# Head of the first mixer: products of the first chunk from x not yet normalized, scaled when they are evicted; squares summed in pairs; the residual parts on VectorE alone

## The chip, the cores and the metric

The kernel runs on one core of a Trainium2 chip. A time is the device time of one execution in microseconds (us). One execution is also profiled, and the profile and trace that are read below come from it.

The core's engines work side by side, each through its own queue in order: PE (TensorE, matrix products, with PEld for its weight loads), DVE (VectorE), ACT (ScalarE), POOL (GpSimd) and SP, which here issues the DMA transfers. Matrix products are written to PSUM, of which there are eight banks.

## The reference

One inference step of a two-layer hybrid decoder: a Mamba-2 layer with an MLP, then a layer of sliding-window attention with an MLP. 1024 prompt tokens, 8x8 sample tokens and 16 meta tokens go through with shared weights. Only the start of the first layer matters here:

```python
def rmsnorm(x, w):
    xf = x.astype(jnp.float32)
    xf = xf * lax.rsqrt(jnp.mean(xf * xf, axis=-1, keepdims=True) + EPS)
    return (xf * w.astype(jnp.float32)).astype(x.dtype)

def mamba_mixer(h, conv_state, ssm_state, norm_w, w_in, conv_w, conv_b, dt_bias, ...):
    zxbcdt = rmsnorm(h, norm_w) @ w_in
    z = zxbcdt[..., :D_INNER]
    xbc = zxbcdt[..., D_INNER:D_INNER + CONV_DIM]
    dt_raw = zxbcdt[..., D_INNER + CONV_DIM:]
    ...
    for k in range(CONV_K):
        conv = conv + xpad[:, k:k + L] * conv_w[k]
    xbc = jax.nn.silu(conv)
    ...
```

The factor rsqrt(...) is one number per token. With features on the partitions and tokens on the columns, as the kernel has it, it is one number per column, the same for all features, and so it can be taken into x ahead of the product or into the product's columns afterwards.

## The kernel before

All 1104 tokens lie on the columns, in three chunks: `CH = [(0, 384), (384, 384), (768, 336)]`, chunk 2 being the last prompt tokens with the sample and meta tokens. Features lie on the 128 partitions in `KT = 8` tiles. Every product of fp32 matrices is made from three: each operand is split into a high part (cast to fp32r on ACT, `xh`, `wh`) and a low part (the rest, by a subtraction, `xl`, `wl`), and PE sums `wh xh + wh xl + wl xh` over k. So one unit of 128 output features takes 24 matmuls a chunk.

The mixer works group by group (8 groups). A group has four convolution units, B, C, x0 and x1. `conv_unit` loads a unit's weights into a `raw` buffer (two) and splits them into `w` buffers (six), and has an `xp` buffer (two) and an `fm` buffer (eight, which the pieces of x use too). `conv_mm` and `conv_mms` make the products in PSUM banks `g` (three), `conv_out` evicts them on ACT into `xp` and, scaled by the convolution's last weight, into `fm`. `conv_rest` does the rest of the convolution and its silu: small copies on POOL, three steps over the 80 tail columns and three over 1024 columns on DVE, Tanh on ACT. The dt product (`dt_product`) feeds `dt_path`, a chain on DVE and ACT whose results the scan (`ssd`) of every group needs.

The function `mixer` is the head that is changed. It loads chunk 2, the weights of B and C, chunk 0, chunk 1. For each chunk `sums_x` squares x on ACT and sums over the partitions with an f32 product against a matrix of 1/D on PE (chunk 2 adds the two squares of a pair on DVE first, chunks 0 and 1 give each square to PE); `rstd_x` makes exp(-0.5 ln(.)) on ACT; `norm_x` scales x in place on DVE (line 354), casts the high part on ACT (L355) and subtracts on DVE and POOL in turn (L357). `conv_mms` then makes B's and C's products of the chunk (L569 to L571), chunk 2 first. After the three chunks come the dt product (L436, L437), x0's products (L205 to L207, the helper `mm3`), `conv_rest` of B, C and x0, `dt_path` (its first transposes on PE at L466), x1, and the scan.

The order in every engine's queue is not written out: a planner orders the instructions by the program's order as priority and its own estimate of when each is ready. `issue_after(i)` adds an edge: what is traced in its block is queued behind instruction i on i's engine. Buffers of a pool go round: an instruction whose tile has no free buffer waits for the last reader of an older one. Besides `g`, PSUM holds one bank each of the tags `cb`, `st` and `tp` and two of `y`; the small SBUF pools are `n1` (five) and `n3` (two, where the rsqrt rows lie).

Of the kernel before, what the change touches and what calls it, by code (L numbers as in the profile page):

```python
# [3 lines left out]

# [5 lines left out]
F32 = mybir.dt.float32  # L10
F32R = mybir.dt.float32r
AF = mybir.ActivationFunctionType
ALU = mybir.AluOpType
# [4 lines left out]
P = 128  # L18
D = 1024
KT = D // P  # L20
# [8 lines left out]
CH = [(0, 384), (384, 384), (768, 336)]  # L29
CORD = [2, 0, 1]  # L30
# [112 lines left out]
class Kernel:  # L143
# [132 lines left out]
    def consts(self):  # L276
        nc, i = self.nc, self.i
        self.cp = cp = self.pool("const")
        self.ident = cp.tile([P, P], F32, name="ident")
        make_identity(nc, self.ident)  # L280

        ones = cp.tile([P, P], F32R, name="ones_r")
        nc.vector.memset(ones.bitcast(F32), 1.0 / D)
        self.ones_r, self.ones_d = ones, ones.bitcast(F32)
        eps = cp.tile([P, 3], F32, name="eps")
        self.eps1, self.eps4, warm = (eps[:, k:k + 1] for k in range(3))
        nc.vector.memset(self.eps1, EPS)

        nc.scalar.activation(out=warm, in_=self.eps1, func=AF.Ln)
        nc.vector.memset(self.eps4, 4.0 * EPS)  # L290
        self.nv = cp.tile([P, KT, 8], F32, name="nv")
        nc.sync.dma_start(out=self.nv, in_=i["nv"])

    def ncol(self, r):
        return self.nv[:, :, r]
# [26 lines left out]
    def sums_x(self, c, hp, tag, add=False):  # L322

        nc = self.nc
        n = CH[c][1]
        ms = self.psa.tile([P, 512], F32, tag=tag, bufs={"y": 2}.get(tag, 1), name="xms")
        for kp, h in enumerate(hp):
            sq = [self.n1("xsq")[:, :n] for _ in range(2)]
            for j in range(2):
                nc.scalar.activation(out=sq[j], in_=h[:, j], func=AF.Square)  # L330
            if add:
                nc.vector.tensor_tensor(out=sq[0], in0=sq[0], in1=sq[1], op=ALU.add)
            for j in range(1 if add else 2):
                nc.tensor.matmul(out=ms[:, :n], lhsT=self.ones_d, rhs=sq[j], start=(kp + j == 0),
                                 stop=(kp == 3 and (add or j == 1)))
        return ms[:, :n]

    def rstd_x(self, mss):
        rs = [self.n3()[:, 0, :ms.shape[1]] for ms in mss]
        for r, ms in zip(rs, mss):  # L340
            self.nc.scalar.activation(out=r, in_=ms, func=AF.Ln, bias=self.eps1)
        for r in rs:
            self.nc.scalar.activation(out=r, in_=r, func=AF.Exp, scale=-0.5)
        return rs

    def norm_x(self, c, hp, rs):

        nc = self.nc
        n = CH[c][1]
        w = self.ncol(5)  # L350
        xh, xl = self.xparts(c)
        for k in range(KT):
            h = hp[k // 2][:, k % 2]
            nc.vector.scalar_tensor_tensor(out=h, in0=h, scalar=w[:, k:k + 1], in1=rs, op0=ALU.mult, op1=ALU.mult)
            nc.scalar.copy(out=xh[:, k], in_=h)  # L355
            e = nc.gpsimd if k % 2 else nc.vector
            e.tensor_tensor(out=xl[:, k], in0=h, in1=xh[:, k].bitcast(F32), op=ALU.subtract)  # L357
        return xh, xl


# [197 lines left out]
                 [(xs[c][0][:, k, :n], xs[c][1][:, k, :n]) for k in range(KT)])  # L558
        self.conv_out(unit, c, pt)

    def conv_mms(self, units, c, xs):

        n = CH[c][1]
        pts = [self.gps() for _ in units]
        mm = partial(self.nc.tensor.matmul, skip_group_check=True)
        for k in range(KT):
            xh, xl = (x[:, k, :n] for x in xs[c])
            for (j, (wh, wl), *_), pt in zip(units, pts):
                mm(out=pt[:, :n], lhsT=wh[:, k], rhs=xh, start=(k == 0), stop=False)  # L569
                mm(out=pt[:, :n], lhsT=wh[:, k], rhs=xl, start=False, stop=False)  # L570
                mm(out=pt[:, :n], lhsT=wl[:, k], rhs=xh, start=False, stop=(k == KT - 1))  # L571
        for unit, pt in zip(units, pts):
            self.conv_out(unit, c, pt)

    def conv_out(self, unit, c, pt):
# [1376 lines left out]
    def mixer(self, c1):  # L1952

        nc = self.nc
        mp = self.pool("mixc", ctx=c1)
        self.sp = self.pool("sp", ctx=c1)
        self.psa = self.pool("psa", bufs=1, space=PSUM, ctx=c1)
        xs, fm = {}, {}
        hp = {2: self.load_h(2)}
        us = [self.conv_unit(0, nm) for nm in ("B", "C")]  # L1960
        hp[0] = self.load_h(0)
        hp[1] = self.load_h(1)
        self.mixer_consts(mp)
        ms2 = self.sums_x(2, hp[2], "cb", True)
        rs2 = self.rstd_x([ms2])[0]
        xs[2] = self.norm_x(2, hp[2], rs2)
        ms0 = self.sums_x(0, hp[0], "st")
        ms1 = self.sums_x(1, hp[1], "y")
        self.conv_mms(us, 2, xs)
        rs0, rs1 = self.rstd_x([ms0, ms1])  # L1970
        for c, rs in ((0, rs0), (1, rs1)):
            xs[c] = self.norm_x(c, hp[c], rs)
            self.conv_mms(us, c, xs)
        draw = self.dt_product(mp, xs)
        ux = self.conv_unit(0, "x0")
        fm["B"], fm["C"] = (self.conv_rest(u) for u in us)
        for c in CORD:
            self.conv_mm(ux, c, xs)
        fm["x0"] = self.conv_rest(ux)
        sums = self.dt_path(mp, draw)  # L1980
        next(sums)
        ux = self.conv_unit(0, "x1")
        for k, c in enumerate(CORD):
            if k == 1:
                next(sums, None)
            self.conv_mm(ux, c, xs)
        next(sums, None)
        fm["x1"] = self.conv_rest(ux)
        for g in range(G):
            gate = None  # L1990
            if g + 1 == G:
                y = [self.fm([P, T], "gy") for j in range(2)]
                space = lambda c: ((self.sp.tile([P, 1024], F32, tag="bm", bufs=1, name="gt") if c == 1 else
                                    self.cw.tile([P, T], F32, tag="th", bufs=1, name="gt"))[:, :768]
                                   .rearrange("p (j n) -> p j n", j=2))
                gate = self.gate_group(0, xs, y, space, lambda: self.fm([P, T], "gm"))
            for t in self.ssd(g, fm):
                for k in range({8: 2, 2: 1, 3: 1, 6: 1, 7: 1}.get(t, 0) if gate is not None else 0):
                    next(gate)
            if g + 1 < G:  # L2000
                fm = self.group_in(g + 1, xs)
        nc.sync.dma_start(out=self.o["conv"], in_=self.cvo)
        for _ in gate:
            pass
        return xs
# [68 lines left out]
```

## Time and profile before

| | |
|---|---|
| time, median of three executions | 2864.05 us (2859.41 to 2864.07) |
| profiled execution | 2867.18 us, of which its span (first to last instruction) is 2865.5 us |
| granted TensorE clock | 0.992 |
| PE busy | 2800.5 us (98%) |
| DVE busy | 2077.3 us (72%) |
| ACT busy | 1419.1 us (50%) |
| POOL busy | 472.0 us (16%) |
| DMA | 433.41 MB, 151 GB/s mean |

A row of a timeline gives start and length, engine, line of the kernel, operation, the tiles written and read with their shapes, how many instructions are merged, and in brackets the idle time of the engine before it and what released it. A row of a group gives busy time and the mean length in ns, then the idle time ahead of the group. Matmuls are pipelined, so the length of one contains latency; its price is the step from one start to the next. "L569" is line 569 of the kernel before.

### The profile page before, as it was taken

Reading aid. Unit: us, or ns where it says so; the run is one execution under the profiler, and the core shown is the slowest. Engines: PE = TensorE matmul, PEld = TensorE weight load, DVE = VectorE, ACT = ScalarE, POOL = GpSimd, SP = SyncE. Lnnn points to the kernel's source line nnn. Section 1 sums busy time; section 2 is a strip of 40 time slices with the busy share of each in tenths; the row PEclk is TensorE's granted clock in tenths of the full one; section 3 lists DMA queues with packets and bytes.
Section 4 is the critical chain, followed back from the end, with each engine's and each line's share of the span. In section 5 each row is a group of like instructions: output and inputs, shape, how many; then the busy total and the mean of one; then the engine's idle time right before and its main releaser. Section 6 shows DMA issues by size and latency. Waiting matters only on the chain.

```text
span 2865.5 us, 51402 instructions
## 1 busy us (share of the span) xinstructions
PE 2800.5 (98%) x19895; PEld 2697.7 (94%) x19895; DVE 2077.3 (72%) x3615; ACT 1419.1 (50%) x2742; POOL 472.0 (16%) x659
## 2 busy tenths in 40 slices
PE   8999999989999999999999999999999999999998
PEld 6999999979999999999999999988989999999997
DVE  6788888876778786666578875676687666567786
ACT  6555555554664265445344335555555455523333
POOL 3255555551000100000000022110110000000011
PEclk9999999999999999999999999999999999999998
DMA  4244444457655223533655523446553454533432
GB/s 139 77 133 124 122 124 124 125 142 249 244 204 184 88 94 130 178 132 131 248 192 181 187 94 92 165 170 245 175 194 105 143 174 152 219 115 127 143 114 70
DMA packets 219468, 433.41 MB, mean 151 GB/s; under 512 B 30729, under 2 KB 128393, under 8 KB 216649
## 3 DMA queue, kind: packets, MB, share of 16 engines
q1 hardware_dynamic: 219224, 430.14, 45.2%
q8 instruction: 156, 2.56, 0.4%
q14 instruction: 88, 0.71, 0.1%
HBM read 302.71 MB, written 128.32 MB: 150 GB/s over the span
## 4 chain that ended last, share of the span: by engine, by line
PE 84%; DVE 7%; DMA 5%; ACT 3%; issue 2%; POOL 0%; SPq 0%; DVEq 0%; ACTq 0%; POOLq 0%
PE g L205 11%; PE g L206 11%; PE g L207 11%; PE mc L205 4%; PE mc L207 4%; PE mc L206 4%; PE ma L205 4%; PE ma L207 4%; PE ma L206 4%; PE md L206 3%; PE md L207 3%; PE md L205 3%; PE mb L206 3%; PE mb L205 3%; PE mb L207 3%
## 5 line engine op out<-in xcount | busy, mean ns | idle before, releaser
L205 PE MATMUL g<-S,w 128*128 128x384 f32 (+2 forms) x1584 | 530.0, 335 | 3.7 <-DMA w<-ws_up 1.9
L206 PE MATMUL g<-S,w 128*128 128x384 f32 (+2 forms) x1584 | 531.3, 335 | 0.0
L207 PE MATMUL g<-S,w 128*128 128x384 f32 (+2 forms) x1584 | 527.2, 333 | 0.0
L1068 ACT CAST w<-s 128x384 fp32r<-128x384 f32 (+1 forms) x272 | 150.3, 557 | 318.0 <-PE mc L207 57.7
L205 PEld LDWEIGHTS g<-S,w 128*128 128x128 f32 x1584 | 298.4, 188 | 6.7 <-issue 3.4
L206 PEld LDWEIGHTS g<-S,w 128*128 128x128 f32 x1584 | 298.9, 189 | 3.0 <-issue 2.4
L207 PEld LDWEIGHTS g<-S,w 128*128 128x128 f32 x1584 | 299.4, 189 | 2.1 <-issue 1.7
L1319 POOL TENSOR_TENSOR hh<-hh,us 128x552 f32<-128x552 f32 (+1 forms) x24 | 42.4, 1788 | 1535.9 <-DVE us L1295 880.4
L205 PE MATMUL ma<-S,w 128*128 128x276 f32 (+1 forms) x808 | 234.3, 290 | 5.8 <-ACT A L1256 2.1
L206 PE MATMUL ma<-S,w 128*128 128x276 f32 (+1 forms) x808 | 234.0, 290 | 0.4 <-DVE S L1257 0.3
L207 PE MATMUL ma<-S,w 128*128 128x276 f32 (+1 forms) x808 | 234.1, 290 | 0.0
L1069 DVE TENSOR_TENSOR w<-s,w 128x384 fp32r<-128x384 f32 (+1 forms) x272 | 166.3, 615 | 77.8 <-ACT w L1068 77.8
L1068 ACT CAST w<-raw 128x384 fp32r<-128x384 f32 (+1 forms) x204 | 112.2, 556 | 177.0 <-PE mc L207 55.7
L171 ACT CAST w<-raw 128x1024 fp32r<-128x1024 f32 x96 | 100.7, 1049 | 136.0 <-PE g L206 47.4
L205 PEld LDWEIGHTS ma<-S,w 128*128 128x128 f32 x808 | 152.6, 189 | 6.7 <-ACT A L1256 2.2
L206 PE MATMUL g<-R,w 128*128 128x384 f32 (+2 forms) x480 | 158.3, 330 | 0.0
L205 PE MATMUL g<-R,w 128*128 128x384 f32 (+2 forms) x480 | 157.8, 329 | 0.0
L207 PE MATMUL g<-R,w 128*128 128x384 f32 (+2 forms) x480 | 157.7, 329 | 0.0
L172 DVE TENSOR_TENSOR w<-raw,w 128x1024 fp32r<-128x1024 f32 x96 | 121.5, 1266 | 45.2 <-ACT w L171 30.8
L206 PEld LDWEIGHTS ma<-S,w 128*128 128x128 f32 x808 | 152.9, 189 | 0.8 <-DVE S L1257 0.5
L207 PEld LDWEIGHTS ma<-S,w 128*128 128x128 f32 x808 | 152.8, 189 | 0.0
L205 PE MATMUL mc<-S,w 128*128 128x276 f32 (+1 forms) x512 | 148.1, 289 | 0.7 <-DVE rx L1098 0.7
(497 smaller groups left out, 8559.8 us busy)
## 6 DMA issues: line engine op xcount, KB each, us to landing
raw<-in_w_up_dram SPq DMA_DIRECT2D x64, 512.0 KB
raw<-in_w_in_dram SPq DMA_DIRECT2D x48, 512.0 KB
raw<-in_w_downs_dram SPq DMA_DIRECT2D x64, 384.0 KB
w<-ws_o SPq DMA_DIRECT2D x46, 512.0 KB
w<-ws_q SPq DMA_DIRECT2D x40, 512.0 KB
ab<-acs_d SPq DMA_DIRECT2D x64, 256.0 KB
S<-t_d SPq DMA_DIRECT2D x18, 828.0 KB
S<-t_e SPq DMA_DIRECT2D x18, 816.0 KB
```

Source lines behind the costliest of these rows:

```text
L171: nc.scalar.copy(out=wh, in_=raw)
L172: nc.vector.tensor_tensor(out=wl, in0=raw, in1=wh.bitcast(F32), op=ALU.subtract)
L205: mm(out=out, lhsT=wh, rhs=xh, start=(first and k == 0), stop=False)
L206: mm(out=out, lhsT=wh, rhs=xl, start=False, stop=False)
L207: mm(out=out, lhsT=wl, rhs=xh, start=False, stop=(k == n - 1))
L1068: self.last_hi = nc.scalar.copy(out=t[:, 0], in_=src).ins
L1069: self.last_lo = nc.vector.tensor_tensor(out=t[:, 1], in0=src, in1=t[:, 0].bitcast(F32), op=ALU.subtract).ins
L1319: e.tensor_tensor(out=to, in0=to, in1=uv, op=ALU.add)
```

## The change

- `ln_exp`, new, issues one load of the activation table that holds both Ln and Exp at the start of ACT's queue.
- `raw_x`, new, makes the high and low parts of chunk 2 from x times the norm's weight alone, without the rsqrt: Identity with a scale on ACT, one scalar_tensor_tensor on DVE, for each of the eight feature tiles.
- B's and C's products of chunk 2 are made from these parts in the two `y` banks (`held`) and are not evicted at once. When rs2 is there, DVE multiplies each by it into an `n1` tile, which `conv_out` reads in place of PSUM.
- All three chunks sum the pairs of squares on DVE before the f32 product. The sums lie in the banks `cb`, `st` and `tp`. Chunk 0 goes first; chunks 2 and 1 share one `rstd_x`.
- `norm_x` subtracts on DVE alone, and scaling k is queued behind subtraction k-2 on DVE.
- Chunk 2 is normalized after all for the later products, behind chunk 1's last subtraction on DVE.
- x0's products come before the dt product and in the order of chunks 0, 1, 2; `conv_rest` of B and C stands between them and the dt product.

```diff
@@ consts
+        self.ln_exp()
         nc.scalar.activation(out=warm, in_=self.eps1, func=AF.Ln)
@@
+    def ln_exp(self):
+        nc = self.nc
+        return nc.scalar.add_instruction(mybir.InstLoadActFuncSet(
+            name=nc.get_next_instruction_name(), engine=mybir.EngineType.Activation, act_func_set_id=6,
+            ins=[], outs=[])).ins
@@ sums_x
-        ms = self.psa.tile([P, 512], F32, tag=tag, bufs={"y": 2}.get(tag, 1), name="xms")
+        ms = self.psa.tile([P, 512], F32, tag=tag, name="xms")
@@
-    def norm_x(self, c, hp, rs):
-        nc = self.nc
-        n = CH[c][1]
+    def raw_x(self, c, hp):
+        nc = self.nc
         w = self.ncol(5)
         xh, xl = self.xparts(c)
         for k in range(KT):
             h = hp[k // 2][:, k % 2]
-            nc.vector.scalar_tensor_tensor(out=h, in0=h, scalar=w[:, k:k + 1], in1=rs, op0=ALU.mult, op1=ALU.mult)
-            nc.scalar.copy(out=xh[:, k], in_=h)
-            e = nc.gpsimd if k % 2 else nc.vector
-            e.tensor_tensor(out=xl[:, k], in0=h, in1=xh[:, k].bitcast(F32), op=ALU.subtract)
+            nc.scalar.activation(out=xh[:, k], in_=h, func=AF.Identity, scale=w[:, k:k + 1])
+            nc.vector.scalar_tensor_tensor(out=xl[:, k], in0=h, scalar=w[:, k:k + 1], in1=xh[:, k].bitcast(F32),
+                                           op0=ALU.mult, op1=ALU.subtract)
+        return xh, xl
+
+    def norm_x(self, c, hp, rs):
+        nc = self.nc
+        n = CH[c][1]
+        w = self.ncol(5)
+        xh, xl = self.xparts(c)
+        subs = []
+        for k in range(KT):
+            h = hp[k // 2][:, k % 2]
+            with self.tc.issue_after(subs[k - 2]) if k > 1 else nullcontext():
+                nc.vector.scalar_tensor_tensor(out=h, in0=h, scalar=w[:, k:k + 1], in1=rs, op0=ALU.mult, op1=ALU.mult)
+            self.last_cast = nc.scalar.copy(out=xh[:, k], in_=h).ins
+            subs.append(nc.vector.tensor_tensor(out=xl[:, k], in0=h, in1=xh[:, k].bitcast(F32), op=ALU.subtract).ins)
+        self.last_side = subs[-1]
         return xh, xl
@@
-    def conv_mms(self, units, c, xs):
+    def conv_mms(self, units, c, xs, pts=None):
         n = CH[c][1]
-        pts = [self.gps() for _ in units]
+        hold = pts is not None
+        pts = pts or [self.gps() for _ in units]
...
-        for unit, pt in zip(units, pts):
+        for unit, pt in zip(units, () if hold else pts):
             self.conv_out(unit, c, pt)
@@ mixer
-        ms2 = self.sums_x(2, hp[2], "cb", True)
-        rs2 = self.rstd_x([ms2])[0]
-        xs[2] = self.norm_x(2, hp[2], rs2)
-        ms0 = self.sums_x(0, hp[0], "st")
-        ms1 = self.sums_x(1, hp[1], "y")
-        self.conv_mms(us, 2, xs)
-        rs0, rs1 = self.rstd_x([ms0, ms1])
-        for c, rs in ((0, rs0), (1, rs1)):
-            xs[c] = self.norm_x(c, hp[c], rs)
-            self.conv_mms(us, c, xs)
+        xs[2] = self.raw_x(2, hp[2])
+        rs0 = self.rstd_x([self.sums_x(0, hp[0], "cb", True)])[0]
+        held = [self.psa.tile([P, 512], F32, tag="y", bufs=2, name="xy") for _ in us]
+        self.conv_mms(us, 2, xs, held)
+        ms2 = self.sums_x(2, hp[2], "st", True)
+        xs[0] = self.norm_x(0, hp[0], rs0)
+        self.conv_mms(us, 0, xs)
+        ms1 = self.sums_x(1, hp[1], "tp", True)
+        rs2, rs1 = self.rstd_x([ms2, ms1])
+        n = CH[2][1]
+        for unit, pt in zip(us, held):
+            t = self.n1("xy")[:, :n]
+            nc.vector.tensor_tensor(out=t, in0=pt[:, :n], in1=rs2, op=ALU.mult)
+            self.conv_out(unit, 2, t)
+        xs[1] = self.norm_x(1, hp[1], rs1)
+        self.conv_mms(us, 1, xs)
+        with self.tc.issue_after(self.last_side):
+            xs[2] = self.norm_x(2, hp[2], rs2)
+        ux = self.conv_unit(0, "x0")
+        for c in range(3):
+            self.conv_mm(ux, c, xs)
+        fm["B"], fm["C"] = (self.conv_rest(u) for u in us)
         draw = self.dt_product(mp, xs)
-        ux = self.conv_unit(0, "x0")
-        fm["B"], fm["C"] = (self.conv_rest(u) for u in us)
-        for c in CORD:
-            self.conv_mm(ux, c, xs)
         fm["x0"] = self.conv_rest(ux)
```

More of the change, by code (lines that the diff above doesn't have):

```diff
@@ L1 @@
-from contextlib import ExitStack, contextmanager
+from contextlib import nullcontext, ExitStack, contextmanager
 from functools import partial
@@ L342, in rstd_x @@
         for r in rs:
-            self.nc.scalar.activation(out=r, in_=r, func=AF.Exp, scale=-0.5)
+            self.last_exp = self.nc.scalar.activation(out=r, in_=r, func=AF.Exp, scale=-0.5).ins
         return rs
+    def raw_x(self, c, hp):
[8 more added lines that the diff above has]
+        return xh, xl
     def norm_x(self, c, hp, rs):
```

## The prediction

> **What bounds the kernel now.** I read the busy line of the page first, then the busy time by stage, then the order of time of the first 76 us, engine by engine. In the stage rows the columns are the length, then PE, PEld, DVE, ACT and POOL with instruction counts, the granted clock, the DMA share and GB/s.
>
> ```profile
> span 2865.5 us, 51402 instructions
> PE 2800.5 (98%) x19895; PEld 2697.7 (94%) x19895; DVE 2077.3 (72%) x3615; ACT 1419.1 (50%) x2742; POOL 472.0 (16%) x659
> 0.00:10.60 10.60, 4.33 (x7) 2.25 (x8) 2.49 (x8) 5.96 (x11) 4.35 (x27) 1.00 0.79 268
> 10.60:21.40 10.80, 6.18 (x19) 2.73 (x17) 9.12 (x13) 10.51 (x23) 3.91 (x4) 1.00 1.00 354
> 21.40:34.40 13.00, 13.00 (x64) 10.60 (x65) 7.83 (x13) 9.96 (x21) 5.27 (x7) 1.00 0.16 52
> 34.40:55.50 21.10, 18.11 (x98) 16.54 (x97) 14.91 (x26) 13.02 (x26) 11.07 (x16) 1.00 0.14 50
> 55.50:75.80 20.30, 20.30 (x123) 18.52 (x120) 13.96 (x14) 9.36 (x17) 3.52 (x8) 1.00 0.23 78
> 75.80:110.00 34.20, 34.20 (x217) 33.54 (x218) 26.98 (x44) 16.60 (x36) 4.84 (x12) 1.00 0.24 56
> 110.00:600.00 490.00, 489.94 (x3347) 449.92 (x3346) 402.58 (x693) 271.18 (x641) 261.19 (x371) 1.00 0.46 125
> 600.00:660.00 60.00, 52.31 (x356) 43.32 (x356) 43.45 (x99) 30.40 (x82) 30.33 (x37) 0.91 0.55 146
> ```
>
> PE is the bound, and from 55.5 to 600 us it never rests. So a microsecond by which PE's stream starts earlier in the head is a microsecond of the total, as long as what feeds PE afterwards keeps up. The head is what is left: up to 55.5 us PE is busy for 41.6 of 55.5 us, and part of that is slow or removable work. Its marks in order of time (start, length, engine and line, and in brackets the idle time before and its releaser):
>
> ```profile
> 4.56 1.78 ACT L330 ACTIVATE xsq<-xt 128x336 f32<-128x336 f32 x4 [2.26 <-DMA xt<-in_x_dram]
> 7.43 1.79 ACT L330 ACTIVATE xsq<-xt 128x336 f32<-128x336 f32 x4 [1.09 <-DMA xt<-in_x_dram]
> 9.55 1.04 ACT L171 CAST w<-raw 128x1024 fp32r<-128x1024 f32 x1 [0.33 <-DMA raw<-in_w_in_dram]
> 10.62 2.54 DVE L172 TENSOR_TENSOR w<-raw,w 128x1024 fp32r<-128x1024 f32 x2 [0.86 <-ACT w L171]
> 14.48 0.48 ACT L343 ACTIVATE n<-n 128x336 f32<-128x336 f32 x1
> 15.00 5.22 DVE L354 SCALAR_TENSOR_TENSOR xt<-xt,nv,n 128x336 f32<-128x336 f32 x8 [1.56 <-ACT n L343]
> 21.40 0.42 PE L570 MATMUL g<-S,w 128*128 128x336 f32 x1 [1.91 <-DVE S L357]
> 36.03 0.44 PE L570 MATMUL g<-S,w 128*128 128x384 f32 x1 [1.28 <-DVE dx L478]
> 40.76 0.44 PE L569 MATMUL g<-S,w 128*128 128x384 f32 x1 [0.60 <-ACT fm L584]
> 46.66 0.44 PE L570 MATMUL g<-S,w 128*128 128x384 f32 x1 [1.11 <-DVE S L357]
> 55.51 0.31 PE L436 MATMUL g<-S,w 128*64 128x336 f32 x1
> ```
>
> The first chunk (336 columns) has landed by 7.4 to 9 us, and B's weights are cast by 10.6. Yet its products run only from 21.4, because sum, Ln, Exp, scaling and split stand between. The products of the three chunks and the remaining sums then take until 55.5, where the dt product starts (L436).
>
> **The change part by part.** Prices of PE work first, from starts that follow each other:
>
> ```profile
> 21.66 0.32 PE L571 MATMUL g<-S,w 128*128 128x336 f32 x1
> 21.82 0.32 PE L570 MATMUL g<-S,w 128*128 128x336 f32 x1
> 25.57 0.81 PE L334 MATMUL xms<-xsq,ones_r 128*128 128x384 f32 x2
> 26.37 0.81 PE L334 MATMUL xms<-xsq,ones_r 128*128 128x384 f32 x2
> 55.16 0.34 PE L570 MATMUL g<-S,w 128*128 128x384 f32 x1
> L334 PE MATMUL xms<-xsq,ones_r 128*128 128x384 f32 x32 | 12.7, 495 | 2.7 <-ACT xsq L330 2.7
> L334 PE MATMUL xms<-xsq,ones_r 128*128 128x336 f32 x8 | 4.9, 760 | 6.3 <-DVE xsq L332 6.3
> ```
>
> A product of 336 columns steps by 0.155 us, one of 384 by 0.175 (two of them from 55.16 to the 55.51 above). A sum over squares is one f32 product, two records; from 25.57 to 26.37 there are one of these and one 336 product in 0.80, so it costs 0.645 (384), by columns 0.56 (336).
>
> *Raw products (raw_x, held).* For chunk 2, eight Identity activations take the place of the eight squares at 4.56 to 9.2, and eight DVE subtractions follow them; both are done by about 10. So PE starts at 9.55+1.04 = 10.6 with 48 products of 0.155, 7.4 us; C's cast and the second halves of both weights (13.2) come before PE needs them.
>
> *Sums paired.* Before, 20 f32 products: 4 for chunk 2, 8 each for the others. After, 12: 4x0.56+8x0.645 = 7.4 us of PE, of which none lies ahead of 10.6 any more. The eight extra additions go to DVE.
>
> *Chunks 0 and 1.* 96 products of 0.175 = 16.8 us, as before.
>
> *Cold start.* The first eight sum records, the narrower ones, average 760 ns, against 495x336/384 = 433 by columns of the later ones: 1.75 times slower, though the granted clock column says 1.00. They fill the 4.3 busy us ahead of 10.6, which were free. After the change the first PE work is on the path: 4.33x(1-1/1.75) = 1.9 us lost. Bounds: 0 if the slowness is only waiting between records, 4.3 if it lasts twice as long; I take 1.9, what the rows themselves give.
> The Trainium skill, "TensorE: Matmul & The Clock Gate" ("What's actually happening"), speaks against the change here: whatever is issued in roughly the first 3.4 us of matmul activity runs at half the clock. By it the loss is an estimated 1.7 us instead of 1.9; the rows agree in kind, the clock column does not show it.
>
> *The normalizing path.* Before, a chunk's parts alternate between DVE and POOL; after, all lie on DVE, 16 instructions a chunk in a fixed order.
>
> ```profile
> 28.91 6.60 DVE L354 SCALAR_TENSOR_TENSOR xt<-xt,nv,n 128x384 f32<-128x384 f32 x8 [5.17 <-ACT n L343]
> 39.81 4.32 DVE L354 SCALAR_TENSOR_TENSOR xt<-xt,nv,n 128x384 f32<-128x384 f32 x8 [1.47 <-ACT n L343]
> 44.16 4.62 POOL L357 TENSOR_TENSOR S<-xt,S 128x384 fp32r<-128x384 f32 x4
> 35.43 0.54 DVE L357 TENSOR_TENSOR S<-xt,S 128x384 fp32r<-128x384 f32 x1
> L357 DVE TENSOR_TENSOR S<-xt,S 128x384 fp32r<-128x384 f32 x8 | 7.3, 952 | 0.0
> ```
>
> The same eight scalings took 6.60 us with POOL's subtractions beside them and 4.32 before POOL's began at 44.16. So 0.54 each without POOL, and 0.54 for a subtraction: 1.08 per k, against six products of 0.175 = 1.05 on PE. Bounds 0.54 and 0.95 per instruction (DVE's mean beside POOL); I take 0.6, near the low end, since no such POOL work is left, plus a little for waiting on the cast.
> The Trainium skill, "SBUF — State Buffer" ("Who interferes with whom"), says that a DVE instruction with two SBUF inputs and a GpSimd one that reads SBUF exclude each other. By it the price is 0.54, and the two L354 rows agree; I keep 0.6.
>
> When does it start? Chunk 0 lands at about 14.0: ahead of its end 32+1344+1024+1536 KB (4.03 MB) are queued by their shapes, 2.84 MB have moved by 10.6 (268 GB/s), the rest at 354. Behind the last piece come its two squares (1.0) and what took chunk 2 from its last square (9.22) to its Exp's end (14.96), 5.7, less two weight casts (2.1) and the table load (1.3): 17.3, and 18 with PE's queue ahead of the last sum. DVE then has 32x0.6 = 19.2, four additions for chunk 1 (0.5 each), x0's weight subtraction (1.2), two scalings of the held products (1.0) and a pause of about 1 between the chunks (rs1 needs rs0's buffer, then Ln and Exp): 42.4.
>
> *Sum to the end of chunk 1.* PE: 10.6+1.9+7.4+7.4+16.8 = 44.1, with its own stalls on top: 0 (x0's first chunk fills them) to 6 (twice the 3.0 us of the rows at 36.03, 40.76 and 46.66). I take 2, as DVE ends at 42.4, just ahead. So 46.1 against 55.5: 9.4 us gained.
>
> *Table loads.* One load at the start takes the place of those between Ln and Exp:
>
> ```profile
> L343 ACT ACT_TABLE_LOAD x3 | 3.8, 1283 | 0.1
> L341 ACT ACT_TABLE_LOAD x2 | 2.6, 1283 | 0.0
> 62.50 1.13 ACT L606 ACTIVATE th<-fm 128x1104 f32<-128x1104 f32 x1 [1.10 <-DVE fm L603]
> ```
>
> Five of 1.28 us go; the first Tanh may need a new one. On rs0's chain two would have counted, but PE is busy with chunk 2 and sums until about 22 (10.6+1.9+7.4+2.6), so the gain is in the cover and counts as nothing; at the Tanh ACT idles 1.10.
>
> *x0 ahead of dt, normalizing chunk 2 late.* The dt product and x0 change places; same work. x0's load passes w_dt's on SP's queue: w_dt is needed 20 us later than x0, nothing lost. Chunk 2's true parts cost DVE 16x0.55 = 8.8, to 51; x0 reaches its third chunk at 46.1+8.4 = 54.5, so this is covered by 3 us. What is queued behind it on DVE is conv_rest of B (the first two rows are of the chain of waits: the dt product's last step and the transposes behind x0):
>
> ```profile
> 63.50 0.18 PE g L437
> 75.79 2.04 PE tp L466 x18
> 58.71 4.87 DVE L603 SCALAR_TENSOR_TENSOR fm<-xp,cv,fm 128x1024 f32<-128x1024 f32 x4
> 76.72 1.23 DVE L172 TENSOR_TENSOR w<-raw,w 128x1024 fp32r<-128x1024 f32 x1 [6.79 <-ACT w L171]
> ```
>
> Three tail steps (0.3 each) and three of 1.2: B's xp is free at 55.6, and only then can x0's evictions start (two xp buffers) and give back a PSUM bank. PE needs a bank again when x0's third chunk is through, at 54.5+3.7 = 58.2. Cover 2.6 us. DVE idled 6.8 us ahead of 76.72, so its backlog of some 7 us can be worked off. I put 0.4 for this passage, bounds 0 and 5.
>
> *Total.* 9.4-0.4 = 9.0. The profiled execution took 2867.2 us (span 2865.5), 3.1 above the median of 2864.05; so 2858 like it, 2855 as a median. With bounds: best 9.4+2+1.9 = 13.3 gained, worst 9.4-4-2.4-5 = -2.0.
>
> **The rivals.**
> *DVE becomes the bound.* If its instructions cost 0.82 (the contended L354 row), chunks 0 and 1 end at 18+26.2+5.2 = 49.4, chunk 2's parts at 61, B's conv_rest at 65.6, and the dt product, waiting for a bank, runs from 66.2 for its 8 us (55.5 to 63.7 before) to 74, where before both were through at 75.8: gain 2, time 2862. For it: DVE is at 72% over the run; against: the 4.32 row.
> *Later stages give it back.* Group 0's dt path and scan are chains through DVE, ACT and DRAM; with PE ahead, PE may wait where it did not. DVE is busy 26.98 of 34.2 us there. Then the gain shrinks to between 0 and 4: 2862. Against: PE waits nowhere from 55.5 to 600, and dt is also ready earlier. The stretch from 600 to 660 does have 7.7 us of idle PE, and the order of all queues is planned anew.
> *Slower: the bank ring locks.* x0 holds all three g banks until conv_rest of B, behind chunk 2's 16 instructions on DVE, lets go of xp; the dt product needs a bank. Past 58.2 us every microsecond of B's conv_rest is PE idle; it decides from 58.2+9.4 = 67.6, and to lose 0.2% it must end at 73.3. That takes 0.98 per DVE instruction over the 48 of three chunks (55.6+48x0.37), about the 952 mean beside POOL. With it 2871.
> *The table load does not take.* If Ln and Exp still load their tables, rs0 comes 2.6 us later, at 20.6, still ahead of 22, but DVE ends at 45 and 1 more us shows: 2856.
>
> **How the numbers follow.** Likeliest, 0.58: 2855, its own range 2851 to 2859. DVE-bound 0.14, given back 0.14, slower 0.09, table loads kept 0.05. About 0.2% (5.7 us) is what can be told from no change: faster means below 2858.3. Of the likeliest case nine tenths lie there, all of the kept loads, and little of the two 2862 cases: 0.52+0.05+0.03 = 0.60. Slower 0.09, the rest 0.31. The range 2849 to 2864 takes in the two middle rivals and leaves out the slow one and the best corner.
>
> **What would show it.** Right: L569 to L571 from about 10.6, the first of them slow; no L357 on POOL; 12 sums (24 records) at L334's successor; one table load ahead of the first Exp; the dt product behind x0, and the transposes after it (L466) at about 66 instead of 75.8. Wrong: PE idle between 22 and 58 above 6 us, DVE instructions in the norm above 0.7 us, or an idle PE waiting for ACT's eviction of x0 before the dt product; or the head ends 9 us earlier but the span does not.

## The result: 0.2% slower, and the profile after

| | changed kernel | before, beside it |
|---|---|---|
| time, median | 2868.09 us (2863.84 to 2873.16, 15 executions) | 2862.69 us (2855.85 to 2868.49, 15 executions) |
| ratio, 95% interval | 1.0022 [1.0014, 1.0029] | |
| profiled execution | 2865.91 us, span 2864.2, clock 0.992 | 2867.18 us, span 2865.5 |

The forecast was 2855, 9 us won; measured are some 4 to 6 us lost (a second series, below, gave 1.0013). The profiled execution of before happened to be one of its long ones, so the two spans say nothing; the medians and the place where time goes do. Lines of the changed kernel stand further down: L592 to L594 are L569 to L571 of before, L342 is L334, L376 to L378 are L354 to L357, L458 and L459 are L436 and L437, L603 to L607 are `conv_out`, L626 is L603, L1073 is L1050 and L1056 is L1033. In the experiments the lines stand up to five off these again (in e5 L348 and L350 are Ln and Exp, in e8 L1991 is the added products).

Two lines of the page of the changed kernel, and its busy time by stage, with the columns as in the prediction:

```profile
span 2864.2 us, 51383 instructions
PE 2791.4 (97%) x19879; PEld 2692.9 (94%) x19879; DVE 2083.2 (73%) x3645; ACT 1418.2 (50%) x2746; POOL 451.0 (16%) x647
```

```profile
10.60:21.40 10.80, 10.47 (x46) 8.98 (x47) 6.12 (x9) 7.89 (x17) 0.72 (x3) 1.00 0.98 351
21.40:34.40 13.00, 13.00 (x62) 10.31 (x62) 11.73 (x25) 11.12 (x26) 2.67 (x7) 1.00 0.15 52
34.40:55.50 21.10, 18.68 (x104) 17.59 (x103) 18.89 (x43) 14.91 (x33) 0.61 (x4) 1.00 0.16 52
55.50:75.80 20.30, 18.37 (x104) 15.87 (x103) 18.04 (x19) 11.19 (x18) 3.46 (x10) 0.92 0.23 76
2175.00:2200.00 25.00, 16.55 (x98) 16.25 (x97) 23.01 (x27) 14.21 (x20) 0.00 (x0) 0.80 0.27 88
```

PE is busy for 9.1 us less than before, and the head does start earlier: 10.47 of 10.8 us busy where it was 6.18. But from 55.5 to 75.8, where PE had never rested, it now lacks 1.9 us and its clock falls to 0.92. And at 2175 to 2200 us, in a stage that the change doesn't touch, PE stands for 8.45 of 25 us. The same stretch of before:

```profile
2175.00:2200.00 25.00, 24.94 (x168) 24.72 (x168) 25.00 (x28) 18.22 (x24) 0.00 (x0) 1.00 0.13 45
```

Counted at one mark after another, the lead over before is 2.9 us at the first scan (first row of L508 of before at 99.9 us, 97.1 after), 8.2 when the last `g` product before 2192 starts, and is gone when the first `ma` product follows (2191.5 before, 2192.0 after).

The head of the changed kernel in order of time, from its timelines:

```profile
10.59 0.65 PE L592 MATMUL xy<-S,w 128*128 128x336 f32 x1 [10.59 <-ACT w L171]
14.54 0.48 PE L594 MATMUL xy<-S,w 128*128 128x336 f32 x1
15.09 0.32 PE L593 MATMUL xy<-S,w 128*128 128x336 f32 x1
16.08 0.56 DVE L340 TENSOR_TENSOR xsq<-xsq 128x384 f32<-128x384 f32 x1 [0.59 <-ACT xsq L338]
20.43 0.81 PE L342 MATMUL xms<-xsq,ones_r 128*128 128x384 f32 x2
21.51 0.56 ACT L349 ACTIVATE n<-xms,eps 128x384 f32<-128x384 f32 x1
23.28 1.14 DVE L376 SCALAR_TENSOR_TENSOR xt<-xt,nv,n 128x384 f32<-128x384 f32 x2
39.45 0.61 PE L592 MATMUL g<-S,w 128*128 128x384 f32 x2 [2.21 <-ACT S L377]
46.52 0.56 DVE L378 TENSOR_TENSOR S<-xt,S 128x384 fp32r<-128x384 f32 x1
60.55 0.32 PE L207 MATMUL g<-S,w 128*128 128x336 f32 x1
60.75 1.04 ACT L171 CAST w<-raw 128x1024 fp32r<-128x1024 f32 x1 [4.80 <-PE g L206]
62.07 0.68 ACT L607 ACTIVATE fm<-g,cv 128x384 f32<-128x384 f32 x1
62.80 0.52 PE L458 MATMUL g<-S,w 128*64 128x336 f32 x1 [1.93 <-ACT fm L607]
66.19 0.36 PE L458 MATMUL g<-S,w 128*64 128x336 f32 x1
64.63 1.28 ACT L629 ACT_TABLE_LOAD   x1
```

PE starts at 10.59, and steps by 0.28 us until about 15. The last pair of chunk 0's squares is added by 16.64, but PE takes its four sums between the products of chunk 2, the last at 20.43, so the scaling starts at 23.28 instead of 18. At 60.7 x0 is through; then the dt product waits 1.93 us for a bank (2.1 from where its start was due), and its next 12 products step by 0.28 again instead of 0.155. Products at such a slow step are called cold below.

The place of the loss, first in the changed kernel, then in the one before (PE, then DVE; L1050 and L1073 evict a bank `g`):

```profile
2183.18 0.34 PE L207 MATMUL g<-S,w 128*128 128x384 f32 x1
2191.97 0.56 PE L205 MATMUL ma<-S,w 128*128 128x272 f32 x1 [8.45 <-DVE n L1073]
2196.18 0.30 PE L205 MATMUL ma<-S,w 128*128 128x272 f32 x1
2187.79 1.29 DVE L1056 TENSOR_TENSOR S<-X,S 128x1088 fp32r<-128x1088 f32 x1
2189.59 0.56 DVE L1073 SCALAR_TENSOR_TENSOR n<-g,acc 128x384 f32<-128x384 f32 x1
2191.26 0.56 DVE L1073 SCALAR_TENSOR_TENSOR n<-g,acc 128x384 f32<-128x384 f32 x1
```

```profile
2191.00 0.34 PE L205 MATMUL g<-S,w 128*128 128x384 f32 x1
2191.54 0.28 PE L205 MATMUL ma<-S,w 128*128 128x272 f32 x1
2198.07 0.55 DVE L1050 SCALAR_TENSOR_TENSOR n<-g,acc 128x384 f32<-128x384 f32 x1
```

Before, `ma` follows on the last `g` product at once; the last eviction at 2198 is of a bank that `ma` doesn't need. After, PE is through at 2183.4, but the two last evictions stand on DVE behind other work until 2191.8, and `ma` needs one of their banks. On top, the 18 products up to 2196.18 step by 0.23 instead of 0.125, 1.9 us more.

### The profile page after: what moved, and what is told of

The parts are those of the page before. It is cut to its first block, busy times and chain, and to the rows that moved or that the text cites. A ratio compares the mean times of both kernels' runs of the same rounds, so it can differ in the third digit from the quotient of the medians.

```text
span 2864.2 us, 51383 instructions
## 1 busy us (share of the span) xinstructions
PE 2791.4 (97%) x19879; PEld 2692.9 (94%) x19879; DVE 2083.2 (73%) x3645; ACT 1418.2 (50%) x2746; POOL 451.0 (16%) x647
## 4 chain that ended last, share of the span: by engine, by line
PE 85%; DVE 5%; DMA 4%; ACT 3%; issue 2%; SPq 0%; DVEq 0%; POOL 0%; ACTq 0%
PE g L205 11%; PE g L206 11%; PE g L207 11%; PE ma L205 4%; PE ma L207 4%; PE ma L206 4%; PE mc L205 4%; PE mc L207 4%; PE mc L206 4%; PE md L206 3%; PE md L207 3%; PE md L205 3%; PE mb L205 3%; PE mb L206 3%; PE mb L207 3%
## 5 line engine op out<-in xcount | busy, mean ns | idle before, releaser
L205 PE MATMUL mc<-S,w 128*128 128x276 f32 (+1 forms) x512 | 148.1, 289 | 0.4 <-DVE hh L1318 0.4
L207 PE MATMUL mc<-S,w 128*128 128x276 f32 (+1 forms) x512 | 147.9, 289 | 0.0
```

The lines of the kernel that those rows point to most:

```text
L205: mm(out=out, lhsT=wh, rhs=xh, start=(first and k == 0), stop=False)
L207: mm(out=out, lhsT=wl, rhs=xh, start=False, stop=(k == n - 1))
```

## The experiments

The theory came from the code of the bank ring. `g` banks are dealt out in turn:

```python
def gps(self):
    pool = self.gring[self.gpos % len(self.gring)]
    self.gpos += 1
    ...
```

The change makes the first two products in `y` banks, `gps` is not called for them, and so `gpos` stays two behind for the rest of the program. In stages where the ring mixes two pools (at 2130 us three banks of one and five of another) each later product falls on another bank; the planner then orders the queues there in another way. The rival was that the loss is in the head: the late scaling, the bank wait, the cold products. All runs stand beside runs of the kernel before on the same chip; ratios are to those.

| run | median us | ratio, 95% interval | wait for `ma` at 2190 |
|---|---|---|---|
| the change | 2868.09 | 1.0022 [1.0014, 1.0029] | 8.45 |
| e0: the change again | 2866.04 | 1.0013 [1.0004, 1.0021] | 8.44 |
| e1: ring position given back | 2855.73 | 0.9980 [0.9972, 0.9989] | none |
| e2: before, position less 2 | 2874.14 | 1.0041 [1.0029, 1.0052] | 8.4 |
| e7: position given back late | 2860.14 | 0.9989 [0.9981, 0.9998] | none |
| e9: given back early, taken late | 2867.39 | 1.0015 [1.0006, 1.0024] | 8.44 |
| e3: e1, dt product ahead of x0 | 2854.09 | 0.9972 [0.9962, 0.9983] | none |
| e4: e1, half the subtractions on POOL | 2861.73 | 0.9999 [0.9989, 1.0008] | none |
| e5: e1 without the table load | 2867.56 | 1.0015 [1.0006, 1.0023] | none |
| e6: e1, chunks 0 and 1 unpaired | 2865.87 | 1.0013 [1.0002, 1.0023] | none |
| e8: e3, PE kept busy from 4.7 us | 2853.26 | 0.9965 [0.9951, 0.9978] | none |

**e0, the change again**, unaltered, for the spread from chip to chip.

> The changed kernel once more, for a second profile. Ring theory (the two products of the first chunk no longer draw a bank from the g ring, so every later product of the program draws another bank, and the planner orders the queues anew where the ring mixes two pools, at 600 to 840 us and 2130 to 2190 us): the wait of 8.5 us that PE has at 2192 us, ahead of the first product of the second MLP's blocks, is there again, between 6 and 10 us, with DVE as its releaser, and the time is 2864 to 2873 us, 1.002 of before. Rival (chance of one execution: pauses and clock windows fall differently each time): the wait is absent or under 3 us in this profile.

The loss is there again, 1.0013, with the same wait. It is 4 to 6 us.

**e1 and e2, the ring position alone.** e1 gives the position back in the change, e2 takes it from the kernel before, with nothing else of the change.

```diff
 # e1, in conv_mms of the change
+        if hold:
+            self.gpos += len(units)
 # e2, in mixer of the kernel before, behind conv_mms(us, 2, xs)
+        self.gpos -= 2
```

> The changed kernel with the ring position advanced by two where the products are held, so that every later product draws the bank that it drew before the change; the head is that of the changed kernel. Ring theory: the wait at 2192 us is gone (under 1.5 us), the stages behind the head are those of before, and the head's lead of 2.9 us (in the first scan at 100 to 120 us) reaches the end: 2860 us, ratio to before 0.9990, between 0.9978 and 1.0000. Rival (the head's change itself costs the time, through the clock or through queues that start in another phase): 2868 us, ratio 1.002 as for the changed kernel.

> The kernel before with the ring position set back by two behind the first chunk's products; its head is untouched. Ring theory: it pays what the later stages pay in the changed kernel without the head's lead: 2871 us, ratio 1.003, between 1.002 and 1.0045, with a wait of some 8 us at 2190 us. Rival (the head costs the time): nothing changes, ratio 1.000 within 0.001.

e1 has no such wait, and 0.9980: the change's head without the shift is 5.7 us (0.2% of 2862) faster than before. Its stretch at 2175:

```profile
2175.00:2200.00 25.00, 24.94 (x173) 24.72 (x172) 25.00 (x28) 16.05 (x22) 0.00 (x0) 1.00 0.19 67
```

In e2 the wait appears in the old kernel. From its list of PE waits between 2190 and 2200 us (line and tile waited for, total us, times, longest):

```profile
PE ma L205 <- DVE n L1050: 8.4, 1, 8.4
```

1.0041 is 11.7 us, for a position in a ring; the rival has no place for that. It agrees with the change's trace, where 8.45 of wait and 1.9 of cold products are 10.3.

**e7 and e9, which stage.** By the order of DVE's and ACT's instructions in the traces, the change's queues differ from e1's at 660 to 890 us, at 2130 to 2200 and in the last stage, from 2820 on. Between 637 and 674 us the changed kernel also seemed to fall back 5.8 us. e7 gives the position back only ahead of the stage at 2130 us; e9 gives it back in the head and takes it away there. Both edits stand at the same line and hold to the end of the program.

```diff
                 self.more_banks(ce, 5, 0)
+                self.gpos += 2        # e7, in the change; e9: -= 2, in e1
                 plain = self.plain_up(1, (0, 1), ...)
```

> The changed kernel as it is, with the ring position advanced by two only ahead of the second layer's plain up-products at 2130 us. Of the two places where the planner's order differs from before, only the later one goes back to before's order; the one at 640 to 840 us stays. Ring theory with both places priced by the profiles (8.5 us of wait at 2192 us and 1.5 us of cold products behind it; 3.6 to 5.8 us between 637 and 674 us): 8 to 10 us less than the changed kernel, 2858 us, ratio 0.999 to 1.000. Rival (the loss is somewhere else and both places only show it): 2866 us, ratio 1.0015.

> The complement of e7: the change with the ring position given back in the head, and taken away again (minus 2) just ahead of the last stage that mixes two pools (about 1640 us). Theory (the two places add up): the wait of 8 us at 2190 is back and the lag between 637 and 674 us is gone; with e1 at 2855.7 and the second place worth 6 to 8 us, 2862 to 2864, ratio 1.000 to 1.0005. Rival (only the second place counts, and e7's remainder was scatter): as the change itself, 2866 to 2868, ratio 1.0015 to 1.002, with the first place back to the change's order by itself of no worth.

e7 has no wait and is 2860; e9 has it (the row below) and is 2867. So what comes behind 2130 us carries the loss by itself. It isn't the last stage: from the last `ma` product of before (2792 us) to the end the change and e9 even gain 0.5 us on before, e1 and e7 nothing.

```profile
2194.65 0.57 PE L205 MATMUL ma<-S,w 128*128 128x272 f32 x1 [8.44 <-DVE n L1075]
```

My theory that the two places add up, the early one with 6 to 8 us, fell. Its lag was mostly a matter of counting. At the sum that ends it (L260, 673.2 before, 674.4 after) the change is 1.2 us behind, but its queue has put 159 products of `g` ahead of that sum since 642.5 us, where before has 134 since 644.9; 25 products of 0.175 are 4.4 us. Counted at a later mark (first `md<-A` product, 917 us), the change, e0 and e7 have lost 1.7 to 2.8 us on before since 611, e1 and e9 0.6 to 1.5. So the early place costs perhaps 1 to 2 us there, and by 2126 us the change is even 7.2 ahead of before, e9 6.0. Such leads are against the one profiled execution of before, whose clock was at half for 10.24 us between 1650 and 2000, where the change's was for 3.41; that alone is 3.4 us. The intervals of e1 and e7 overlap, so what is left for the early place in the time is between nothing and some 6 us.

**e3, x0 and dt product changed back.** On e1:

```diff
-        for c in CORD:                  # dt_product
+        for c in range(3):
@@ mixer
+        draw = self.dt_product(mp, xs)
         ux = self.conv_unit(0, "x0")
+        fm["B"], fm["C"] = (self.conv_rest(u) for u in us)
         for c in range(3):
             self.conv_mm(ux, c, xs)
-        fm["B"], fm["C"] = (self.conv_rest(u) for u in us)
-        draw = self.dt_product(mp, xs)
```

> As the one with the ring position restored, and besides the dt product is put back ahead of x0's products, in the order of chunks 0, 1, 2. It tests the head's bank wait: at 60.7 us PE waited 2.1 us for a bank that x0's first eviction had to give back, and ran the next 12 products at half pace (0.28 instead of 0.155 us). Theory: both go, 3.6 us, so the first scan is 6 to 7 us ahead of before and the time is 2856 us, ratio 0.9977. Rival (PE is only moved from one wait to another, since the normalized chunk 2 is ready only at 59.6 us on DVE): the head's lead stays at 3 us and the time at 2860 us, ratio 0.999.

The bank wait goes, yet the first scan comes at 95.8 as in e1, not 2 us or more earlier as I expected. Behind the scans (637 us) e3 is 3.0 us ahead of e1; in the medians it is 1.6, with overlapping intervals. So the exchange of x0 and dt brought nothing, and may have cost 2 to 3 us.

**e5, the table load.** e1 without `ln_exp()`.

> The changed kernel with the ring position restored, without the load of the joint table at the start, so that Ln and Exp load their tables by turns. Theory of the prediction (the loads lie beside PE's work on the raw products): the head's lead stays within 1 us, 2856 us, ratio 0.998. Rival (on ACT they delay rsqrt, casts and evictions of the chunks): four or five loads of 1.28 us show for 2 us or more, 2858 us or above.

10.8 us are lost at the first scan (106.6 against 95.8 in e1) and 10 in the time (1.0015 against 0.9980; the two ran on different chips, so the ratios are compared). Both expectations were too small. Here is how 1.28 us each become that, in ACT's and PE's timelines and two stages of e5:

```profile
22.63 1.28 ACT L348 ACT_TABLE_LOAD   x1
25.27 1.28 ACT L350 ACT_TABLE_LOAD   x1
40.99 1.28 ACT L348 ACT_TABLE_LOAD   x1
29.31 1.01 PE L593 MATMUL g<-S,w 128*128 128x384 f32 x2 [2.63 <-ACT S L376]
47.11 1.01 PE L593 MATMUL g<-S,w 128*128 128x384 f32 x2 [3.73 <-ACT S L376]
```

```profile
30.00:40.00 10.00, 10.00 (x37) 8.43 (x37) 8.17 (x19) 8.92 (x18) 2.07 (x6) 0.73 0.18 56
40.00:50.00 10.00, 6.27 (x28) 5.65 (x27) 6.14 (x16) 8.77 (x16) 0.61 (x4) 0.79 0.00 0
```

Seven more loads lie between 21 and 45 us. Two stand ahead of each chunk on the chain sum, Ln, Exp, scaling; PE waits 2.6 and 3.7 us (2.2 in all in e1), and with each pause its clock falls, to 0.73 and 0.79 in the rows. Of 20 to 60 us the mean is 0.83 where e1 had 1.00, which is 40x0.17 = 6.8 us. With 4.2 us more waiting (6.4 against 2.2) and 0.9 at a sum this makes 11.9. It is an estimate: 1.0 us of it is low clock inside the pauses, counted twice, and one more slow stretch, from 73.0 to 76.4 us behind the bank wait (1.7), isn't in it.

**e6, sums not paired.** On e1, the `True` of `sums_x(0, ...)` and `sums_x(1, ...)` left out.

> The changed kernel with the ring position restored, and the squares of chunks 0 and 1 given to PE one by one, 8 f32 products more. Theory (PE is the bound in the head, each of these costs 0.645 us on it): 5.2 us of lead lost, so no lead over before or little, 2861 us, ratio 1.000. Rival (PE's waits in the head take them up: 2.2 us at 39.5 and 2.0 at 61 us): 1 to 3 us lost, 2857 to 2859 us.

At the first scan 4.3 us are lost (100.0 against 95.8): eight f32 products of 0.645 are 5.2, so the size was right. By the ratios the time is 9 us higher (4 to 15 by the intervals). Where the rest goes isn't shown. In the scans PE waits more, as the list of e6's PE waits has it in its first row (the second is the head's wait, at 42.7):

```profile
PE st L758 <- DVE h L760: 3.6, 4, 1.1
PE g L594 <- ACT S L377: 3.0, 1, 3.0
```

These are three waits of 1.1 us and one of 0.3 between 230 and 590, where e1 hardly waits. But e4 has the same 3.6 us and still stands level with e1 at the first `ma` product (844.9 us in both). Both change the order of the queues far beyond the head.

**e4, POOL again.** On e1 every second subtraction of `norm_x` goes back to POOL.

```diff
-            subs.append(nc.vector.tensor_tensor(...).ins)
+            e = nc.gpsimd if k % 2 else nc.vector
+            i = e.tensor_tensor(...).ins
+            subs.append(subs[-1] if k % 2 else i)
```

> The changed kernel with the ring position restored, and every second subtraction of norm_x back on POOL. My price: beside POOL the scaling cost 0.82 instead of 0.54 us and POOL's subtraction 1.26 us; two chunks then cost DVE and POOL some 4 to 6 us more ahead of the first scan. Theory (parts on DVE alone are worth something): the head's lead in the scan at 100 to 120 us, 4.2 us with the ring restored, falls to 0 to 2 us, the time rises from 2856 to 2858 to 2860 us. Rival (PE is the bound in the head and the parts have cover): the same time within 1.5 us.

The first scan comes as early as in e1 (95.8), so the loss that I expected there didn't come. By the ratios the time is 5 us higher than e1's, and the profile doesn't show where: its execution is the shorter one (2858.8 us against 2860.0). The price of DVE beside POOL is seen in two pairs of scalings, without and with POOL at work:

```profile
37.01 1.14 DVE L376 SCALAR_TENSOR_TENSOR xt<-xt,nv,n 128x384 f32<-128x384 f32 x2
42.57 1.89 DVE L376 SCALAR_TENSOR_TENSOR xt<-xt,nv,n 128x384 f32<-128x384 f32 x2
```

A pair costs DVE 0.75 us more, and it is spared one subtraction of 0.55. So POOL's help is paid for in full, and leaving it off costs the head nothing.

**e8, the cold start.** e3 with PE kept at work before the first real product:

```diff
+        warm = self.psa.tile([P, 512], F32, tag="tp", name="warm")
+        for k in range(KT):
+            nc.tensor.matmul(out=warm[:, :CH[2][1]], lhsT=self.ones_d, rhs=hp[2][k // 2][:, k % 2], start=True, stop=True)
```

> e3 (ring position given back, dt made ahead of x0) with eight more matmuls ahead of everything else on PE: x of the third chunk, as loaded, times a matrix of ones that is there early, into a bank that nothing reads. They have no use but to keep PE working before the first real product at 10.6. Theory (the first 4.4 us of products go at 0.28 us a step because PE had stood still till then): the products from 10.6 go at 0.155 from the start, 2 us are won, about 2852 in the time, ratio 0.9965. Rival (the slow start is the price of the first products whatever ran before, or the transfers of w set the pace): within 1 us of e3, ratio 0.997.

The mechanism holds: the products go at 0.155 from the fourth on.

```profile
4.73 6.16 PE L1991 MATMUL warm<-xt,ones_r 128*128 128x336 f32 x16 [4.73 <-DMA xt<-in_x_dram]
12.02 0.31 PE L594 MATMUL xy<-S,w 128*128 128x336 f32 x1
12.17 0.31 PE L595 MATMUL xy<-S,w 128*128 128x336 f32 x1
40.00:50.00 10.00, 9.32 (x43) 7.90 (x44) 9.45 (x22) 6.20 (x14) 0.00 (x0) 0.83 0.31 105
```

The worth isn't shown: 0.9965 against e3's 0.9972, overlapping, and in the profile the first scan comes at 98.3, 2.4 us after e3's. What feeds chunk 0 comes no earlier, and PE waits 1.8 us for squares instead of 0.7; the clock then fell after the 2.2 us pause at 40 (last row), which it didn't in e3. e1, e3 and e8 beat both kernels, by 0.2 to 0.35% of before.

## Why the prediction was wrong

**The step that failed is one that isn't in the sum: the bank ring's position in later stages.** Every edit was priced in the head, and `pts = pts or [self.gps() ...]` was taken for two other banks for B and C and nothing more. It also moves all later draws by two places. The rival "later stages give it back" named the order of all queues being planned anew, but looked for it in group 0 and at 600 to 660, and bounded the gain at 0; it could go below. Cost by the trace 10.3 us (8.45 + 1.9), by e2 11.7, by e9 against e1 10.

**In the head**, 9.0 us were forecast and 2.9 to 4.2 reached at the first scan (2.9 in the profile of the change, 4.2 in e1's; in the time e1 is 5.7 ahead, 3.1 to 8.0 by its interval). By the prediction's steps:

| step | forecast | measured |
|---|---|---|
| PE starts | 10.6 | 10.59 |
| cold start | 1.9 us | 13 products in the 4.5 us to 15.09, 0.33 of it waiting: 2.1 us lost |
| scaling of chunk 0 starts | 18 | 23.28 |
| DVE per instruction | 0.6 | rows of 0.55 and 0.61, starts 0.5 apart |
| DVE through with chunk 1 | 42.4 | 47.08 |
| PE's own stalls | 2 | 2.4 from 34.4 to 55.5, and 0.3 at 11.5 |
| x0 ends | 58.2 | 60.7 |
| B's `xp` free | 55.6 | 60.8 |
| bank passage | 0.4 | 2.1, and 1.6 for 12 cold products behind it |
| dt product ends | 66 | 72.4 |
| table loads | 0 | some 10 us, if they had stayed |

- *Start of the scaling.* 5.3 us late. I let the sums of chunk 0 follow their squares "with PE's queue ahead of the last sum", 0.7; the queue has the products of chunk 2 between the sums, 3.8 us from the addition's end (16.64) to the last sum (20.43). That is 3.1 of the 5.3. DVE then took 23.8 us where I had 24.4.
- *x0's end.* PE had other products for most of the delay (it stood 2.2 us at 37), and x0 ended only 2.5 us late. That these 2.5 come from the late scaling is argued, not tested.
- *Cold start.* The size was right. Its upper bound was not: twice 1.9 is 3.7, not 4.3.
- *Bank passage.* The place and the kind were right, and so was the sign that was named, an idle PE waiting for ACT's eviction of x0. The size was not: 0.4, bounds 0 to 5, came to 2.1 of waiting plus 1.6. B's `conv_rest` let go of `xp` only at 60.8: POOL, idle for 22 us, waits until then to write x0's first columns into that buffer (the rows below). This is 5.2 us late, and DVE was 4.7 late already at the end of chunk 1, so by these marks the late scaling comes back here; the cover of 2.6 is used up. The eviction could then have begun at 60.9 and began at 61.70: ahead of it in ACT's queue stands a cast of weights (60.75 above), which had waited 4.80 us for a buffer that x0's products still read. So some 0.8 of the 2.1 us are ACT's queue, the rest is DVE. The prediction asked what is queued behind waiting instructions on DVE, but not on ACT.

```profile
59.54 2.48 DVE L626 SCALAR_TENSOR_TENSOR fm<-xp,cv,fm 128x1024 f32<-128x1024 f32 x2
60.98 2.24 POOL L615 COPY xp<-cv 128x24 f32<-128x24 f32 x1 [22.04 <-DVE fm L626]
61.70 0.47 ACT L603 COPY xp<-g 128x384 f32<-128x384 f32 x1
```

- 9.0 - 2.5 - 1.7 - 1.6 = 3.2, against 3.4 where x0 and the dt product are both through (75.8 before, 72.4 after).
- *Table loads.* "The gain is in the cover and counts as nothing" was wrong in the other direction: e5 lost 10 us by them. PE had cover for time, but not for the pauses and the low clock that comes with them. The rival that priced kept loads at 1 us was mis-sized tenfold. Since the sum was built from PE work alone, it contained this gain without naming it: a PE that never waits is what the loads would have prevented.
- *DVE becomes the bound, and the slow rival of a locked ring* (0.82 or 0.98 per DVE instruction) didn't come by its condition: the price was 0.55. DVE was late all the same, by its late start. That normalizing on DVE alone costs the head nothing holds (e4).

**Of the pauses.** What a short wait costs varies. The same wait of 1.93 us for x0's bank was followed by slow products in the change, e7 and e5, not in e0, e1 and e9; the 2.2 us at 37 to 40 in e0 and e8, not in the five other profiled executions that have it. One of each, the change and e0, from 62 to 68 us:

```profile
62.00:68.00 6.00, 5.20 (x23) 4.22 (x24) 4.99 (x7) 5.45 (x10) 2.20 (x8) 0.72 0.26 87
```

```profile
62.00:68.00 6.00, 4.07 (x26) 3.25 (x25) 5.21 (x6) 5.67 (x10) 1.98 (x8) 1.00 0.27 87
```

The clock records of the twelve traces show an order in this. In each trace all stretches at half clock before 2800 us start on one grid of 3.41 us and last one, two or three of its cells: 3.41 us behind the wait at 62 (62.86 to 66.27), and 10.24 us at 2190, begun inside the pause (2185.95 to 2196.19, of which 4.2 us fall on products). What counts is how much of a pause falls into one cell. The 1.93 us of the change (60.87 to 62.80) lie whole in the cell ahead of 62.86; e1's (61.09 to 63.02) are cut at 62.88, with 1.79 us ahead of the cut, and nothing follows. Before 2800 us every cell with 1.86 us or more of idle PE, 61 in all, is followed by one at half clock; with less it happens sometimes.

The Trainium skill, "TensorE: Matmul & The Clock Gate" ("What's actually happening"), gives a window of about 3.4 us, free-running, both for falling and for rising. The grid of 3.41 us agrees; that a pause must fill a window does not: 1.93 us were enough here.

## What to carry to other kernels

Before a change to one stage is priced, look for what it moves besides its own work: a counter that deals out banks or buffers is state that every later stage reads, and when a planner orders the queues, a shift of two can cost more, 2 ms later, than the change wins (here 10 to 12 us against 6). Give such a counter back its value (one line, e1) before judging the change itself. And price a PE pause at its length plus the slow products behind it, and ask of every queue, ACT's too, what stands behind an instruction that waits.

## What had not been expected of the hardware

- A pause of about 2 us is sometimes followed by 12 products at 0.28 us instead of 0.155, and which one is follows in these traces from how the pause lies on the grid of 3.41 us; the 8.45 us were followed by 18 products at 0.23 instead of 0.125.
- At PE's first work the granted clock column shows 1.00 while products step by 0.28 (10.59 to 15); with eight products ahead of them (e8) they step by 0.155 from 12.02. The change's trace has no clock record before 15.07 us, and the column shows 1.00 where there is none. So it can't be used to rule out a cold start.
